# Two of four feed-forward half steps in seven block products for eight

## The chip, the cores and the metric

The kernel runs on one core of a Trainium2 chip. The metric is device microseconds of one execution. TensorE multiplies matrices out of SBUF into PSUM (eight banks of 128 partitions x 2 KB); VectorE, ScalarE and GpSimd work on tiles in SBUF, the first two on PSUM as well; the DMA engines move data between HBM and SBUF. The engines run side by side and wait for each other by semaphores. A framework places the buffers, sets the waits and fixes each engine's order of instructions before the run; an instruction written later in the program can be placed before one written earlier if its inputs are there sooner.

## The reference

Two layers over 544 tokens (512 of a prompt, 8 x 4 of samples), width D = 1024, feed-forward width 2816. Each layer does

```
x = x + 0.5 * SwiGLU_a(RMSNorm(x))
x = x + Mixer(RMSNorm(x))          # layer 0: mLSTM, layer 1: chunk MLP
x = x + 0.5 * SwiGLU_b(RMSNorm(x))
SwiGLU(x) = (silu(x @ w_gate) * (x @ w_up)) @ w_down
```

and a final RMSNorm follows. All in float32. The four SwiGLU half steps are ffn1 and ffn2 of layers 0 and 1; the change touches ffn1 of layer 0 (the first work of the kernel) and ffn2 of layer 1 (the last).

## The kernel before

x lies in SBUF as eight feature tiles of 128 partitions x 544 tokens. For accuracy each matmul operand is split exactly into a high and a low float32r part (`split_into`, L202: ScalarE writes the high part, VectorE subtracts it for the low part), and a product takes three matmuls: high by high, high by low, low by high (`mm3`, L182). PSUM holds a product as two halves of 272 tokens, so each weight block of 128 x 128 makes six matmuls of 272 columns.

`weight` (L146) loads a piece of 128 x 1024 (512 KB) into one of six `raw` slots and splits it into `whi` and `wlo`, two slots each (`WSP`). The norm's gain is multiplied into x before the split (`prep`, L222), squares are summed on ScalarE and GpSimd (`prep_sq`), and the rows' factor `rstd` is applied behind the products (`prep_end`, L236).

`ffn` (L250) goes through 22 hidden tiles in three groups of 8, 8 and 6 (`FF_GROUPS`). For each tile: gate product (48 matmuls), up product (48), then t = gate * rstd on VectorE (L277), SiLU on ScalarE (L278), times rstd on GpSimd (L279), times up on VectorE (L280), and the split of the hidden tile h (L281). Behind a group come eight down products over its tiles; each is added into x (L294), and in the last group x is made ready for the next block (L297). ffn2 of layer 1 ends in `last_down` (L301) and `finish` (L337), which run the last group of down, the final norm and the output. Between the two layers' halves stand `mlstm` (L378), two further half steps with parts of the sample group's state update in between (L1063), and `chunk_mlp` (L970).

PSUM is one pool: two tiles of two banks (`mm`) and four of one bank (`s`). At the start `run` (L1125) loads x, interleaves the first weight piece with it, and splits tile by tile.

Of the kernel before, what the change touches and what calls it, by code (L numbers as in the profile page):

```python
# [17 lines left out]
NT = 544          # 512 prompt tokens, then 8 x 4 sample tokens  # L18
# [26 lines left out]
# columns of the packed per-feature vectors  # L45
# [4 lines left out]
# columns of the packed shape constants  # L50
# [32 lines left out]
def _host(inp):  # L83
# [8 lines left out]

    a = {}
# [6 lines left out]
    for n in ("ffn1", "ffn2"):  # L100
        for w in ("gate", "up", "down"):
            v = f[f"{n}_w_{w}"]
            a[f"{n}_{w}"] = np.stack([wm(v[0]), wm(v[1])])
# [26 lines left out]
class Trunk:  # L130
# [4 lines left out]
    def pool(self, name, bufs=1, space=None):  # L135
        if space is None:
            return self.tc.tile_pool(name=name, bufs=bufs)
        return self.tc.tile_pool(name=name, bufs=bufs, space=space)

# [6 lines left out]
    def weight(self, src=None, raw=None, parts=1):  # L146
        """Loads a piece of a weight matrix and splits it exactly into two float32r parts."""
# [34 lines left out]
    def mm3(self, ps, hi, lo, k0, xs):  # L182
        """ps[half] = sum_k W[k]^T X[k] with both operands in two parts."""
# [10 lines left out]
    def split(self, pool, tag, src, scale=None, n=NT):  # L194
        """Two float32r tiles that sum to src (times a column)."""
# [40 lines left out]
    def prep_end(self):  # L236
# [3 lines left out]
        for h in range(2):  # L240
            c = slice(h * HN, (h + 1) * HN)
            ps = self.st()[:, :HN]
# [7 lines left out]
    def ffn(self, name, l, nextc, side=(), first=None):  # L250
        nc = self.nc
        a = self.a
        with self.pool("ffn") as fp:
# [8 lines left out]
            for gi, (j0, j1) in enumerate(FF_GROUPS):  # L262
                hs = []
                for j in range(j0, j1):
                    gh, gl = first if j == 0 and first else self.weight(a[name + "_gate"][l, j])
# [4 lines left out]
                    uh, ul = self.weight(a[name + "_up"][l, j])  # L270
# [15 lines left out]
                for m in range(KD):  # L286
                    if lastg and nextc is None:
                        self.last_down(a[name + "_down"][l, m][:, j0:j1, :], hs, m)
                        continue
                    dh, dl = self.weight(a[name + "_down"][l, m][:, j0:j1, :])  # L290
# [10 lines left out]
    def last_down(self, src, hs, m):  # L301
        nc, o = self.nc, self.o
        parts = ((0, 256), (256, NT)) if m == KD - 1 else ((0, NT),)
        dh, dl = self.weight(src)
# [5 lines left out]
        x, yt = self.x[m], self.yt  # L310
        if m < KD - 1:
            self.mm3(ps, dh, dl, 0, hs)
        for pi, (t0, t1) in enumerate(parts):
            c = slice(t0, t1)
            if m == KD - 1:
                pv, xv = ps[:, pi, :t1 - t0], x[:, c]
                for k, (xh, xl) in enumerate(hs):
                    for q, (w, h) in enumerate(((dh, xh), (dh, xl), (dl, xh))):
                        nc.tensor.matmul(out=pv, lhsT=w[:, k * P:(k + 1) * P], rhs=h[:, c],
                                         start=k == 0 and q == 0, stop=k == len(hs) - 1 and q == 2)  # L320
            else:
                pv, xv = ps[:, :, :HN], self.v2(x)
# [14 lines left out]
    def finish(self, pi, t0, t1, sq):  # L337
        """The tokens t0 to t1: the rows' sums on the partitions, their factors back across them, the product."""
        nc, o, fin, yt = self.nc, self.o, self.fin, self.yt
        w = (P, 96)[pi]  # L340
# [30 lines left out]
    def dense(self, out, w, i):  # L371
        """out[p, (n d)] = w[p, i, d] where p // 4 == n."""
# [5 lines left out]
    def mlstm(self, nextc):  # L378
        md = self.md
        with self.pool("mlc") as mc:  # L380
# [22 lines left out]
    def phase_a(self):  # L403
        nc, a, o, con = self.nc, self.a, self.o, self.con
        mmt, st = self.mmt, self.st
        with self.pool("pa") as pa:
            self.qkv = pa.tile([P, 3, NI, 4], F32, name="qkv")
            nc.sync.dma_start(out=self.qkv, in_=a["qkv"])
            # the blocks of W_q W_k^T
# [8 lines left out]
            # gate weights through the block-diagonal projections  # L418
# [31 lines left out]
            def post(i, xm):  # L450
# [3 lines left out]
                # causal convolution  # L454
# [19 lines left out]
                # gates  # L474
# [6 lines left out]
                # v and k, tokens on the partitions  # L481
# [23 lines left out]
            def sample(h):  # L505
                """The sample group's q, k and v of a head: rows (feature tile, token), then q and k turned."""
# [30 lines left out]
    def gate_rows(self, pa, gp):  # L537
# [24 lines left out]
        # log sigmoid  # L562
# [39 lines left out]
        # the sample group's values, four times over on the partitions  # L602
# [75 lines left out]
    def norm_cols(self, nq, ecol, stats, n, m):  # L678
        """Columns of the mean of ps and of 1 / std(h) / den, h = ps / den, den = max(|nq|, ecol)."""
# [445 lines left out]
    def run(self):  # L1125
        nc, a, o = self.nc, self.a, self.o
        with self.pool("com") as com, self.pool("xg", 16) as xg, self.pool("hp", 16) as hp, self.pool("wp") as wp, \
# [68 lines left out]
```

## Time and profile before

| | |
|---|---|
| median of 3 runs | 2337.63 us (2336.07 to 2338.55) |
| profiled execution, span | 2334.9 us |
| TensorE, weight loads, VectorE, ScalarE, GpSimd busy | 99%, 95%, 48%, 34%, 15% |
| the four half steps' matmuls | 4 x 3168 of 18076 |

The span runs from the first to the last instruction of one profiled execution; the runs' times have a few microseconds around it. Busy shares are of the span; TensorE's weight loads run beside its matmuls. Read first which engine is full, then whether the chain of work that ended last runs through it, then stretch by stretch whether it waits.

### The profile page before, as it was taken

How to read it: one execution, taken by the hardware profiler on the slowest of the kernel's cores; microseconds unless marked ns; L12 is line 12 of the kernel's file. 1: busy time of each engine (PE TensorE's matmuls, PEld its weight loads, DVE VectorE, ACT ScalarE, POOL GpSimd, SP SyncE). 2: the span in 40 equal slices, each digit the busy share in tenths (PEclk: the TensorE clock that was granted, in tenths of full speed). 3: DMA queues.
4: the chain of work that ended last, by engine and by line, in shares of the span. 5: the costliest groups of instructions: out<-in, count | busy, mean ns of one | idle time of the engine just before them, and what ended most of it. 6: DMA issues, size and time to landing. Idle time of an engine off the chain costs nothing.

```text
span 2334.9 us, 42078 instructions
## 1 busy us (share of the span) xinstructions
PE 2314.8 (99%) x18076; PEld 2220.8 (95%) x18076; DVE 1126.5 (48%) x1642; ACT 787.8 (34%) x1066; POOL 351.5 (15%) x403
## 2 busy tenths in 40 slices
PE   8999999999999999999999999999999999999998
PEld 8999999988987789999999999999999999999998
DVE  5333336543456676644454454545444644333334
ACT  5222123434455453422222342122233433222123
POOL 1101013332111100210111121011121121001011
PEclk9999999999999999999999999999999999999999
DMA  5322223467767663547563444746333223223221
GB/s 179 90 83 91 91 76 110 152 223 233 247 214 259 237 192 102 173 157 265 157 212 118 139 148 157 264 157 210 119 102 96 70 82 91 90 83 91 91 71 59
DMA packets 131089, 337.50 MB, mean 145 GB/s; under 512 B 13168, under 2 KB 26304, under 8 KB 130904
## 3 DMA queue, kind: packets, MB, share of 16 engines
q1 hardware_dynamic: 101152, 276.52, 36.7%
q0 software_dynamic: 9200, 34.02, 4.5%
q10 hardware_dynamic: 20552, 24.29, 2.9%
q8 instruction: 142, 2.33, 0.4%
q14 instruction: 43, 0.35, 0.0%
HBM read 274.97 MB, written 59.81 MB: 143 GB/s over the span
## 4 chain that ended last, share of the span: by engine, by line
PE 95%; DVE 2%; DMA 2%; ACT 1%; issue 0%; POOL 0%; SPq 0%; DVEq 0%; ACTq 0%
PE mm L191 83%; PE mm L926 2%; PE s L191 2%; PE s L719 1%; PE s L497 1%; PE s L853 1%; PE s L889 1%; PE s L1110 1%; DMA xs<-xsd 1%; DMA raw<-in_ml_down 1%; PE s L1040 0%; PE s L836 0%; DVE wlo L206 0%; PE s L478 0%; DVE wg L424 0%
## 5 line engine op out<-in xcount | busy, mean ns | idle before, releaser
L205 ACT ACTIVATE whi<-raw 128x1024 fp32r<-128x1024 f32 (+2 forms) x345 | 358.0, 1038 | 1296.1 <-PE mm L191 1114.4
L191 PE MATMUL mm<-xgh,whi 128*128 128x272 f32 x3744 | 779.7, 289 | 5.8 <-ACT whi L205 5.8
L191 PE MATMUL mm<-xgl,whi 128*128 128x272 f32 x3744 | 776.1, 288 | 0.4 <-DVE xgl L209 0.4
L191 PE MATMUL mm<-xgh,wlo 128*128 128x272 f32 x3744 | 775.1, 288 | 0.0
L191 PEld LDWEIGHTS mm<-xgh,whi 128*128 128x128 f32 x3744 | 588.3, 188 | 23.8 <-issue 14.1
L191 PEld LDWEIGHTS mm<-xgl,whi 128*128 128x128 f32 x3744 | 587.8, 188 | 0.7 <-DVE xgl L209 0.6
L191 PEld LDWEIGHTS mm<-xgh,wlo 128*128 128x128 f32 x3744 | 587.4, 188 | 0.5 <-issue 0.5
L206 DVE TENSOR_TENSOR wlo<-raw,whi 128x1024 fp32r<-128x1024 f32 (+2 forms) x345 | 413.5, 1199 | 63.0 <-ACT whi L205 49.2
L191 PE MATMUL mm<-hh,whi 128*128 128x272 f32 x1508 | 314.2, 289 | 1.3 <-DVE x L294 1.3
L191 PE MATMUL mm<-hl,whi 128*128 128x272 f32 x1508 | 312.2, 288 | 0.0
L191 PE MATMUL mm<-hh,wlo 128*128 128x272 f32 x1508 | 312.0, 288 | 0.1
L279 POOL TENSOR_TENSOR s<-s,rstd 128x544 f32<-128x544 f32 x88 | 151.8, 1726 | 1002.5 <-ACT s L278 1002.5
L191 PEld LDWEIGHTS mm<-hh,whi 128*128 128x128 f32 x1508 | 236.2, 188 | 6.2 <-issue 6.1
L191 PEld LDWEIGHTS mm<-hh,wlo 128*128 128x128 f32 x1508 | 236.5, 188 | 0.8 <-DVE wlo L206 0.8
L191 PEld LDWEIGHTS mm<-hl,whi 128*128 128x128 f32 x1508 | 236.8, 188 | 0.0
L180 DVE TENSOR_TENSOR t<-mm,s 128x544 f32<-128x544 f32 x83 | 60.1, 725 | 331.6 <-PE mm L191 331.6
L294 DVE SCALAR_TENSOR_TENSOR x<-mm,x 128x544 f32<-128x544 f32 x88 | 63.7, 724 | 249.1 <-PE mm L191 249.1
L277 DVE TENSOR_TENSOR t<-mm,rstd 128x544 f32<-128x544 f32 x88 | 63.6, 724 | 240.5 <-PE mm L191 240.4
L1114 DVE SCALAR_TENSOR_TENSOR c<-c,gib,s 128x512 f32<-128x512 f32 x128 | 88.1, 740 | 0.0
L234 POOL TENSOR_TENSOR acc<-acc,sq 128x544 f32<-128x544 f32 x35 | 56.5, 1614 | 175.7 <-ACT sq L233 175.7
L206 DVE TENSOR_TENSOR hl<-t,hh 128x544 fp32r<-128x544 f32 x88 | 63.2, 718 | 2.9 <-ACT hh L205 2.9
L1116 POOL DMA_DIRECT2D out_Cs<-c x32 | 25.0, 782 | 253.4 <-DVE c L1114 246.6
(304 smaller groups left out, 1763.1 us busy)
## 6 DMA issues: line engine op xcount, KB each, us to landing
raw<-in_ffn_up SPq DMA_DIRECT2D x88, 512.0 KB
raw<-in_ffn_gate SPq DMA_DIRECT2D x87, 512.0 KB
raw<-in_ffn_down SPq DMA_DIRECT2D x64, 512.0 KB
c<-in_sC SPq DMA_DIRECT2D x64, 512.0 KB
c<-in_sC SPq DMA_DIRECT2D x32, 1024.0 KB
out_Cs<-c POOLq DMA_DIRECT2D x32, 1024.0 KB, 6.0
raw<-in_ml_up SPq DMA_DIRECT2D x32, 512.0 KB
raw<-in_ffn_down SPq DMA_DIRECT2D x32, 384.0 KB
```

What stands on the lines that cost most here:

```text
L180: self.nc.vector.tensor_tensor(out=self.v2(out), in0=ps[:, :, :HN], in1=self.v2(by), op=ALU.mult)
L191: nc.tensor.matmul(out=ps[h], lhsT=w[:, wsl], rhs=x[:, h * HN:(h + 1) * HN], start=k == 0 and q == 0, stop=k == n - 1 and q == 2)
L205: nc.scalar.activation(out=hi, in_=src, func=AF.Copy)
L206: nc.vector.tensor_tensor(out=lo, in0=src, in1=hi.bitcast(F32), op=ALU.subtract)
L234: (eng or nc.gpsimd).tensor_tensor(out=self.acc, in0=self.acc, in1=sq, op=ALU.add)
L277: nc.vector.tensor_tensor(out=self.v2(t), in0=psg[:, :, :HN], in1=self.v2(self.rstd), op=ALU.mult)
L279: nc.gpsimd.tensor_tensor(out=s, in0=s, in1=self.rstd, op=ALU.mult)
L294: nc.vector.scalar_tensor_tensor(out=xv, in0=ps[:, :, :HN], scalar=0.5, in1=xv, op0=ALU.mult, op1=ALU.add)
L497: nc.tensor.matmul(out=ps[:, tt * P:(tt + 1) * P], lhsT=t[:, tt * P:(tt + 1) * P], rhs=wd[w], start=True, stop=True)
L926: nc.tensor.matmul(out=ps, lhsT=kk[:, tt], rhs=vv[:, tt], start=tt == 0 and q == 0, stop=tt == 3 and q == 2)
L1114: nc.vector.scalar_tensor_tensor(out=c0[:, r, :], in0=c0[:, r, :], scalar=self.gib[:, h, b:b + 1], in1=ps[r], op0=ALU.mult, op1=ALU.add)
L1116: nc.gpsimd.dma_start(out=self.pair(o["Cs"], v)[:, h, dsl].rearrange("r p e -> p r e"), in_=c0)
```

## The change

Strassen's scheme in Winograd's form. A 2 x 2 block of weight tiles (two feature blocks by two) times a pair of feature tiles is made of seven block products in place of eight. The sums of weight blocks are formed on the chip: B21 + B11 and B21 + B22 by DMAs that add into SBUF (issued on GpSimd, behind a plain load of B21), one on VectorE and one on GpSimd. The sums of x and of the hidden tiles (T1 to T4) are formed on VectorE; all seven are split into high and low parts. The recombination is done in PSUM: a partial result is copied by ScalarE from one bank to another, and later products add to it there; before, eight matmuls with zeros have touched all banks (`arm`). The two token halves play the part of the right operand's columns, so each matmul is still 128 x 128 by 272. PSUM is two sets of four banks in these half steps and the old two kinds elsewhere (`psum`); pools of SBUF tiles change with the stage (`x_pool`). Groups have 3, 3, 3 and 2 blocks (`SV_GROUPS`, a block is two hidden tiles). The last group of down at the very end is done by ordinary products (`last_down`). The first weight piece is no longer loaded ahead of x. The other two half steps, the mLSTM and the chunk MLP keep their work, but for `hp` opened later and one split there.

```diff
+SEVEN = {("ffn1", 0), ("ffn2", 1)}
+SV_GROUPS = ((0, 3), (3, 6), (6, 9), (9, 11))
+ADDS = "dma"
+B11, B21, B22, T4, T1, T2, T3, B12 = range(8)
...
     def prep(self, k):
+        if self.xkind == "s":
+            if k % 2:
+                self.px[k // 2] = self.sums_x(k - 1)
+            self.prep_sq(k)
+            return
...
+    def arm(self):
+        sets = [self.set(), self.set()]
+        for t in sets:
+            for b in range(4):
+                self.nc.tensor.matmul(out=t[:, b, :HN], lhsT=self.onesr, rhs=self.zeros, start=True, stop=True)
+
+    def set(self):
+        return self.pp.tile([P, 4, 512], F32, tag="set", name="set", bufs=2)
+
+    def sums(self, t, hi, lo, parts=1):
+        nc = self.nc
+        nc.vector.tensor_tensor(out=t[:, T1:T3 + 1:2], in0=t[:, B12:B12 + 1].to_broadcast([P, 2, HN]),
+                                in1=t[:, B11:B22 + 1:2], op=ALU.subtract)
+        nc.vector.tensor_tensor(out=t[:, T2], in0=t[:, B22], in1=t[:, T1], op=ALU.subtract)
+        nc.vector.tensor_tensor(out=t[:, T4], in0=t[:, B21], in1=t[:, T2], op=ALU.subtract)
+        for c in ((slice(0, 7),) if parts == 1 else (slice(0, 3), slice(3, 7))):
+            self.split_into(hi[:, c], lo[:, c], t[:, c])
+        return hi, lo
+
+    def sums_x(self, k):
...
+        t = self.ht.tile([P, 8, HN], F32, tag="hT", name="hT", bufs=1)
...
+        return self.sums(t, hi, lo, 2)
+
+    def weight_sums(self, src):
...
+        ta, tb, tc = (raw(self.wp, "raw", 2, RAW) for _ in range(3))
+        td = raw(self.wx, "rawd", 1, 2)
+        nc.sync.dma_start(out=ta[:, 0], in_=b11)
+        if ADDS == "dma":
+            nc.sync.dma_start(out=ta[:, 1], in_=b21)
+            nc.sync.dma_start(out=tc[:, 1], in_=b21)
+            nc.gpsimd.dma_start(out=ta[:, 1], in_=b11, accum_op=ALU.add)
+            nc.gpsimd.dma_start(out=tc[:, 1], in_=b22, accum_op=ALU.add)
+            nc.sync.dma_start(out=tb[:, 0], in_=b12)
+            nc.sync.dma_start(out=tc[:, 0], in_=b22)
...
+        nc.vector.tensor_tensor(out=tb[:, 1], in0=tc[:, 1], in1=ta[:, 0], op=ALU.add)
+        nc.gpsimd.tensor_tensor(out=td[:, 0], in0=tb[:, 1], in1=tb[:, 0], op=ALU.add)
+        out = []
+        for t in (ta, tb, tc):
+            hi, lo = (self.wp.tile([P, 2, 512], F32R, tag=g, name=g, bufs=WSP)[:, :, :n] for g in ("whi", "wlo"))
+            self.split_into(hi, lo, t)
+            out += [(hi[:, i], lo[:, i]) for i in range(2)]
+        hi, lo = (self.wx.tile([P, 512], F32R, tag=g, name=g, bufs=1)[:, :n] for g in ("whd", "wld"))
+        self.split_into(hi, lo, td[:, 0])
+        return out + [(hi, lo)]
+
+    def seven(self, t, src, xs, scale=1.0, sums=None):
+        nc = self.nc
+        w11, w7, w12, w6, w22, w5, w3 = self.weight_sums(src)
+        bank = [t[:, b, :HN] for b in range(4)]
...
+        product(0, w11, B11, True)
+        nc.scalar.activation(out=bank[2], in_=bank[0], func=AF.Copy, scale=-1.0)
+        product(1, w7, T3, True)
+        e = self.wx.tile([P, HN], F32, tag="e", name="e", bufs=2)
+        nc.scalar.activation(out=e, in_=bank[1], func=AF.Copy, scale=scale)
+        product(2, w6, T2, False)
+        nc.scalar.activation(out=bank[3], in_=bank[2], func=AF.Copy)
+        product(0, w12, B21, False)
+        product(3, w5, T1, False)
+        nc.scalar.activation(out=bank[1], in_=bank[3], func=AF.Copy, scale=-1.0)
+        product(2, w22, T4, False)
+        product(1, w3, B22, False)
+        return e.unsqueeze(1).to_broadcast([P, 2, HN])
+
+    def ffn_seven(self, name, l, nextc, start=False):
...
+            for gi, (j0, j1) in enumerate(SV_GROUPS):
+                lastg = gi == len(SV_GROUPS) - 1
+                hs = []
+                for j in range(j0, j1):
+                    t = self.set()
+                    e = self.seven(t, gate[j], xs)
+                    s = ht.tile([P, 2, 2, HN], F32, tag="s", name="s", bufs=1)
+                    u = self.set()
+                    if j == 0:
+                        self.prep_end([u[:, 2, :HN], u[:, 3, :HN]])
+                    r2 = self.v2(self.rstd)
+                    nc.vector.tensor_tensor(out=s[:, 0], in0=t[:, 0:2, :HN], in1=r2, op=ALU.mult)
+                    nc.vector.tensor_tensor(out=s[:, 1], in0=t[:, 2:4, :HN], in1=e, op=ALU.add)
+                    nc.vector.tensor_tensor(out=s[:, 1], in0=s[:, 1], in1=r2, op=ALU.mult)
+                    nc.scalar.activation(out=s, in_=s, func=AF.Silu)
+                    nc.gpsimd.tensor_tensor(out=s.rearrange("p a b c -> p a (b c)"),
+                                            in0=s.rearrange("p a b c -> p a (b c)"),
+                                            in1=self.rstd.unsqueeze(1).to_broadcast([P, 2, NT]), op=ALU.mult)
+                    e = self.seven(u, up[j], xs)
+                    h = ht.tile([P, 8, HN], F32, tag="hT", name="hT", bufs=1)
+                    nc.vector.tensor_tensor(out=h[:, B11:B12 + 1:B12 - B11], in0=u[:, 0:2, :HN], in1=s[:, 0],
+                                            op=ALU.mult)
+                    nc.vector.tensor_tensor(out=h[:, B21:B22 + 1], in0=u[:, 2:4, :HN], in1=e, op=ALU.add)
+                    nc.vector.tensor_tensor(out=h[:, B21:B22 + 1], in0=h[:, B21:B22 + 1], in1=s[:, 1], op=ALU.mult)
...
+                    hs.append(self.sums(h, hi, lo))
...
+                for m in range(KD // 2):
+                    t = self.set()
+                    e = self.seven(t, down[m][:, :, j0:j1], hs, scale=0.5)
...
             self.prep_begin(C_FF1)
-            for k in range(KD):
-                self.px[k] = self.split(self.xg, "xg", self.x[k], scale=self.col(C_FF1 + k))
-                if k == 0:
-                    first = self.weight(raw=raw, parts=2)
...
-            self.ffn("ffn1", 0, C_MIX, first=first)
+            self.psum("s")
+            self.ffn_seven("ffn1", 0, C_MIX, start=True)
+            self.psum("c")
             self.mlstm(C_FF2)
```

## Rows read from the trace of the kernel before

**Rows 1.** The page, part 1: busy time of each engine, share, instructions.

```profile
PE 2314.8 (99%) x18076; PEld 2220.8 (95%) x18076; DVE 1126.5 (48%) x1642; ACT 787.8 (34%) x1066; POOL 351.5 (15%) x403
```

**Rows 2.** The page, part 4: the chain that ended last, by engine.

```profile
PE 95%; DVE 2%; DMA 2%; ACT 1%; issue 0%; POOL 0%; SPq 0%; DVEq 0%; ACTq 0%
```

**Rows 3.** Stretches: PE, PEld, DVE, ACT, POOL busy us, clock, DMA share, GB/s.

```profile
0.00:22.00 22.00, 15.72 (x108) 15.07 (x109) 15.50 (x25) 16.85 (x25) 0.41 (x5) 1.00 0.88 330
148.00:244.00 96.00, 96.00 (x767) 96.00 (x766) 35.50 (x39) 25.37 (x30) 12.39 (x7) 1.00 0.29 88
...
365.00:415.00 50.00, 48.59 (x378) 47.46 (x377) 38.48 (x101) 20.77 (x30) 20.68 (x26) 1.00 0.41 123
```

**Rows 4.** Timeline from 98 us, TensorE and VectorE: start, us, engine, line.

```profile
97.93 0.41 PE L191 MATMUL mm<-xgh,whi 128*128 128x272 f32 x2
...
99.19 0.41 PE L191 MATMUL mm<-xgh,wlo 128*128 128x272 f32 x2
...
99.64 0.72 DVE L277 TENSOR_TENSOR t<-mm,rstd 128x544 f32<-128x544 f32 x1 [3.27 <-PE mm L191]
...
104.96 0.41 PE L191 MATMUL mm<-xgl,whi 128*128 128x272 f32 x2
```

**Rows 5.** Groups by line and shape, whole span: busy us, mean ns, idle before.

```profile
L206 DVE TENSOR_TENSOR wlo<-raw,whi 128x1024 fp32r<-128x1024 f32 x311 | 381.0, 1225 | 62.7 <-ACT whi L205 48.9
L205 ACT ACTIVATE whi<-raw 128x1024 fp32r<-128x1024 f32 x311 | 329.7, 1060 | 1220.6 <-PE mm L191 1068.3 <-issue 75.5 <-DMA raw<-in_ml_up 27.3
...
L277 DVE TENSOR_TENSOR t<-mm,rstd 128x544 f32<-128x544 f32 x88 | 63.6, 724 | 240.5 <-PE mm L191 240.4
...
L208 ACT ACTIVATE xgh<-x,cols 128x544 fp32r<-128x544 f32 x48 | 35.3, 746 | 20.8 <-DVE x L294 11.5 <-DVE x L960 4.6 <-PE mm L191 2.0
L206 DVE TENSOR_TENSOR wlo<-raw,whi 128x768 fp32r<-128x768 f32 x32 | 31.1, 973 | 0.0
L205 ACT ACTIVATE whi<-raw 128x768 fp32r<-128x768 f32 x32 | 27.0, 844 | 75.5 <-PE mm L191 46.0 <-issue 29.3
...
L1116 POOL DMA_DIRECT2D out_Cs<-c x32 | 25.0, 782 | 253.4 <-DVE c L1114 246.6 <-DVE wlo L206 6.8
...
L206 DVE TENSOR_TENSOR hl<-raw,hh 128x512 fp32r<-128x512 f32 x16 | 10.8, 686 | 4.6 <-ACT hh L205 4.6
...
L424 DVE TENSOR_TENSOR wg<-wg,qkv 128x32 f32<-128x32 f32 x48 | 9.9, 268 | 0.0
...
L205 ACT ACTIVATE hh<-raw 128x512 fp32r<-128x512 f32 x16 | 9.3, 625 | 4.4 <-DMA raw<-xsd 3.8 <-ACT sz L675 0.5
...
L245 ACT ACTIVATE rstd<-s,eps 128x272 f32<-128x272 f32 x12 | 5.2, 484 | 0.1
...
L178 DVE TENSOR_TENSOR t<-s 128x272 f32<-128x272 f32 x10 | 3.9, 435 | 8.3 <-POOL s L279 8.3
...
L1101 POOL DMA_DIRECT2D out_ns<-sn x4 | 2.3, 566 | 17.6 <-DVE sn L1099 17.6
```

**Rows 6.** Timeline from 394 us: weights' low parts on VectorE beside GpSimd.

```profile
396.44 0.30 PEld L191 LDWEIGHTS mm<-hh,wlo 128*128 128x128 f32 x2 [0.26 <-DVE wlo L206]
...
400.39 0.95 DVE L206 TENSOR_TENSOR wlo<-raw,whi 128x768 fp32r<-128x768 f32 x1
...
401.95 1.36 POOL L234 TENSOR_TENSOR acc<-acc,sq 128x544 f32<-128x544 f32 x1 [3.59 <-ACT sq L233]
...
402.62 1.50 DVE L206 TENSOR_TENSOR wlo<-raw,whi 128x768 fp32r<-128x768 f32 x1
```

**Rows 7.** Timeline of the start, TensorE and ScalarE.

```profile
5.77 0.82 PE L191 MATMUL mm<-xgh,whi 128*128 128x272 f32 x2 [5.77 <-ACT whi L205]
...
5.98 0.75 ACT L208 ACTIVATE xgh<-x,cols 128x544 fp32r<-128x544 f32 x1 [0.26 <-DMA x<-in_xT]
...
10.14 0.41 PE L191 MATMUL mm<-xgh,whi 128*128 128x272 f32 x2
```

**Rows 8.** The page, part 6: GpSimd's DMAs, KB each, us to landing.

```profile
out_Cs<-c POOLq DMA_DIRECT2D x32, 1024.0 KB, 6.0
```

More of the change, by code (lines that the diff above doesn't have):

```diff
@@ L1 @@
+import contextlib
 import numpy as np
@@ L91, in wm, with pairs @@
         return w.reshape(k // P, P, m // P, P).transpose(2, 1, 0, 3)
+    def pairs(w):
+        k, m = w.shape
+        t = w.reshape(k // 256, 2, P, m // 256, 2, P).transpose(3, 2, 4, 1, 0, 5)
+        return np.stack([t[:, :, i, j] for i, j in ((0, 0), (0, 1), (1, 1), (1, 0))], 2)
     a = {}
@@ L101, in _host @@
         for w in ("gate", "up", "down"):
-            v = f[f"{n}_w_{w}"]
-            a[f"{n}_{w}"] = np.stack([wm(v[0]), wm(v[1])])
+            for l in range(2):
+                a[f"{n}{l}_{w}"] = (pairs if (n, l) in SEVEN else wm)(f[f"{n}_w_{w}"][l])
     a["ml_up"] = wm(f["ml_w_up"][0])
@@ L234, in prep_sq, with prep_end @@
             (eng or nc.gpsimd).tensor_tensor(out=self.acc, in0=self.acc, in1=sq, op=ALU.add)
-    def prep_end(self):
+    def prep_end(self, sums=None):
         nc = self.nc
@@ L241, in prep_end @@
             c = slice(h * HN, (h + 1) * HN)
-            ps = self.st()[:, :HN]
+            ps = sums[h] if sums else self.st()[:, :HN]
             for q in range(2):
@@ L264, in ffn @@
                 for j in range(j0, j1):
-                    gh, gl = first if j == 0 and first else self.weight(a[name + "_gate"][l, j])
+                    gh, gl = first if j == 0 and first else self.weight(a[f"{name}{l}_gate"][j])
                     psg = self.mmt()
@@ L286, in ffn @@
                 for m in range(KD):
[L287 to L290, printed above, removed]
+                    dh, dl = self.weight(a[f"{name}{l}_down"][m][:, j0:j1, :])
                     ps = self.mmt()
@@ new lines, in seven, with product @@
+    def seven(self, t, src, xs, scale=1.0, sums=None):
+        nc = self.nc
+        w11, w7, w12, w6, w22, w5, w3 = self.weight_sums(src)
+        bank = [t[:, b, :HN] for b in range(4)]
+        def product(b, w, i, start):
+            z, last = 0, 3 * len(xs) - 1
+            for k, (xh, xl) in enumerate(xs):
+                c = slice(k * P, (k + 1) * P)
+                for ww, xx in ((w[0], xh), (w[0], xl), (w[1], xh)):
+                    nc.tensor.matmul(out=bank[b], lhsT=ww[:, c], rhs=xx[:, i], start=start and z == 0, stop=z == last,
+                                     skip_group_check=True)
+                    z += 1
+        product(0, w11, B11, True)
[11 more added lines that the diff above has]
+        return e.unsqueeze(1).to_broadcast([P, 2, HN])
@@ L305, in last_down @@
+    def last_down(self, src, m, j0, j1, hs):
+        nc, o = self.nc, self.o
+        parts = ((0, HN), (HN, NT))
+        nj = j1 - j0
+        raw = self.raw(n=2 * nj * P).rearrange("p (a b) -> p a b", a=2)
+        for k in range(2):
+            nc.sync.dma_start(out=raw[:, k], in_=src[:, (0, 1, 3, 2)[2 * (m % 2) + k], j0:j1].rearrange("p a b -> p (a b)"))
+        wh, wl = self.weight(raw=raw.rearrange("p a b -> p (a b)"))
         ps = self.mmt()
@@ L310, in last_down, with half @@
         x, yt = self.x[m], self.yt
+        def half(pi):
+            z = 0
+            for k in range(2 * nj):
+                w0 = (k % 2 * nj + k // 2) * P
+                xh, xl = hs[k]
+                for w, h in ((wh, xh), (wh, xl), (wl, xh)):
+                    nc.tensor.matmul(out=ps[:, pi, :HN], lhsT=w[:, w0:w0 + P], rhs=h[pi],
+                                     start=z == 0, stop=z == 6 * nj - 1)
+                    z += 1
         if m < KD - 1:
-            self.mm3(ps, dh, dl, 0, hs)
-        for pi, (t0, t1) in enumerate(parts):
+            half(0)
+            half(1)
+        for pi, (t0, t1) in enumerate(parts if m == KD - 1 else ((0, NT),)):
             c = slice(t0, t1)
             if m == KD - 1:
[L316 to L320, printed above, removed]
+                half(pi)
+                pv, xv = ps[:, pi, :HN], x[:, c]
             else:
@@ L379, in mlstm @@
         md = self.md
-        with self.pool("mlc") as mc:
+        with self.pool("hp", 16) as self.hp, self.pool("mlc") as mc:
             def dram(shape, name):
@@ L1144, in run @@
             nc.vector.memset(self.eps, EPS)
-            late = com.tile([P, 1], F32, name="late")
-            nc.scalar.activation(out=late, in_=self.eps, func=AF.Copy)
             self.mhalf = com.tile([P, 4], F32, name="mhalf")
```

115 lines of the change are left out of this document (91 added, 24 removed).

## The prediction

> **What bounds the kernel now.** I read the engine totals first, then the chain of work that ended last, then stretches of the span, then single instructions. TensorE is busy 99% of the span while VectorE, ScalarE and GpSimd have 48, 34 and 15% [rows 1], and 95% of the chain is TensorE [rows 2]. Inside a half step nothing waits: in 148 to 244 us TensorE is busy all 96.00 us, VectorE 35.50, GpSimd 12.39, and the DMA engines 0.29 [rows 3]. So a matmul removed there is time removed, as long as the others keep up. The pace: the pairs that start at 97.93 and at 104.96 us lie 56 matmuls apart, 0.1255 us for one [rows 4]. Each matmul already has a weight load of its own, 18076 to 18076 [rows 1], so the same 128x272 form with other weights each time should keep that pace.
>
> **What is removed.** A half step has 3168 matmuls: 22 gate and 22 up tiles of 48, and 8 x 22 x 6 for down. With seven products the gate or up tile pair takes 84 in place of 96, and a down pair of three blocks 63 in place of 72. ffn1 of layer 0 becomes 22 x 84 + 12 x 63 + 4 x 42 = 2772. ffn2 of layer 1 keeps ordinary products for its last two blocks of down: 22 x 84 + 12 x 63 + 192 = 2796. That is 396 + 372 = 768 fewer, times 0.1255 = **-96.4 us**. Zeroing the eight banks twice adds 16 matmuls, **+2**.
>
> **What is added on the other engines, per tile pair of gate and up** (two calls of `seven`, 168 matmuls, 21.1 us of TensorE). Durations from [rows 5]; per element a low part takes (1225 - 686)/512 = 1.05 ns more and a high part 0.85, so 1904 elements are 2.15 and 1.81 us.
> VectorE: weights' low parts 6 x 1.225 + 2 x 0.686 = 8.7; two sums of 512, 1.4; six steps on s and h of 544, 0.72 each, 4.3; the differences of h, 0.72 + 2 x 0.435 = 1.6; h's low part 2.15. Sum **18.2 us** of 21.1, against some 9 of 24.1 now (four weight low parts, six steps of 0.72).
> ScalarE: 6 x 1.06 + 2 x 0.625 = 7.6; eight PSUM copies of 272, between 0.42 (the 512's 0.625 less 240 elements) and the 0.48 of the nearest row, a square root from PSUM, which I take, 3.9; the SiLU of 1088, 1.1; h's high part 1.8. Sum 14.4.
> GpSimd: two sums of 512 (about 1.3 each undisturbed) and a product of 1088, twice the 1.36 that an undisturbed 544 takes [rows 6], so 5.3, and four DMA issues of 0.57 to 0.78 [rows 5].
> DMA: seven pieces of 256 KB for a `seven` in place of four tiles' worth; 1.8 MB in 10.5 us is about twice today's 88 GB/s [rows 3], far from the 330 of the first stretch. I take the traffic as free; the adding DMAs are a rival below.
>
> **One call of `seven`, laid out.** Products start every 12 x 0.1255 = 1.51 us. A result is read 0.2 us behind its slot: the last pair of a product starts at 99.19, its slots end at 99.44, VectorE reads at 99.64 [rows 4]. The third product waits for a ScalarE copy of the first: 0.2 + 0.48 + 0.1 against 1.51, slack 0.7, if ScalarE isn't inside a 1.06 or 1.81 us instruction; the fifth and the seventh wait in the same way for a copy. Each engine's order is fixed before the run and not shown in this trace; behind a waiting copy stand ScalarE's next high parts. The third weight tile takes over the first one's slot (two slots): free at 3.0, high part from 3.1 to 4.2, low part to 5.4, needed at 6.0 to 6.3. Slack under 1 us. Where the gate call runs beside the h chain of the tile pair before, h's high part (1.81) or low part (2.15) lands in one of those slacks and costs 0.5 to 1.6 us; the up call, beside the SiLU and the 2.7 us GpSimd product, about 0.4. A measured relative: in 365 to 415 us, with VectorE at 38.48 of 50 and GpSimd at 20.68, TensorE falls to 48.59, so 2.8% goes [rows 3], in waits on a low part such as the 0.26 at 396.44 [rows 6]. At 86% and with less slack I take 1.7 us for a tile pair, bounds 0.5 and 3.5: 22 x 1.7 = **+37 us** (11 to 77).
> A down call has 1.13 us products, so the copy's slack is 0.3 and the third tile's (0.84 + 0.97 [rows 5]) about 0.2: 0.5 for each of 24 (0.2 to 1); in the last group of ffn1 four calls of 5.3 us carry about 6.8 us of VectorE work, for they also split x: 1.7 each. **+19 us** (6 to 36).
>
> **The end of a group.** Now a group has 8, 8 or 6 tiles, so down begins with 42 or 30 matmuls that don't need the last one. With groups of three, two or so blocks, only 6 (0.75 us) go ahead. Behind the last up product come: read delay 0.2, h 0.72, differences 1.6, high part 1.8, low part 2.15, hand-overs 0.3; 6.8 less 0.75 and a little of the next product leaves 5.7. Nothing else can fill it: both weight slots hold down's first tiles. Seven groups (four in ffn1, three in ffn2; the eighth has no differences): **+40 us** (32 to 49).
>
> **The start.** Now the matmuls run at half pace from 5.77 and in full from about 10 us [rows 7]; 108 in the first 22 us [rows 3] are 13.6 us of work, so it is as if they had begun at 8.4. After: four pairs of x go one behind another through one buffer, each two scaled copies (1.5), differences 1.6, the second high part 1.1, the second low part 1.3 and hand-overs, 5.8 us. The first ends about 5 us behind its second x tile (5.98 [rows 7]), at 11, the fourth at 28.4, and the weights, now queued behind x with an adding DMA on top, come at about 18. By 28.4 some two products (3 us) are done: as if begun at 25.4 to 28 with squares and sums in between. **+20 us** (14 to 25).
>
> **Small ones.** From the chunk MLP into ffn2 the last x pair takes its copies, differences and splits, about 6 us, with 2.2 us of matmuls ahead of it, in place of a cover of 42: +5 (3 to 8). Last down: its first tiles wait for the last h and the banks, +3 (2 to 5). The mLSTM's own weight preparation, of which the 48 steps of 0.27 alone are 9.9 us of VectorE [rows 5], today fills gaps in 365 to 415 us (the 38.48 above) and will meet a full VectorE: +4 (0 to 15). The last chunk-MLP split to another pool: nothing, its slots have long been free.
>
> **Sum.** -96.4 + 2 + 37 + 19 + 40 + 20 + 5 + 3 + 4 = **+33.6 us**. The profiled execution spans 2334.9 us; 2.7 more lie around it up to the median of 2337.63 (runs 2336.07 to 2338.55). I forecast 2334.9 + 33.6 + 2.7 = **2371 us**.
>
> **Rivals.**
> A: the covers hold. All terms at their lower bounds: 11 + 6 + 32 + 14 + 3 + 2 + 0 + 2 = 70, so -26, **2311 us**. For it: an order of work fixed ahead can put the copies and the third tile's split first, and VectorE has 3 us to spare in each tile pair. Against: drain and start alone are 46 of it, and no engine can shorten them.
> B: VectorE and GpSimd shut each other out. A 768 low part takes 0.95 us alone; one that starts at 402.62, while GpSimd adds from 401.95 to 403.31, takes 1.50, as if it had begun when GpSimd ended [rows 6]. Two-input SBUF steps on VectorE are 8.7 + 1.4 + 1.4 + 1.6 + 2.15 = 15.3 of the 18.2; with GpSimd's 5.3 they fill 20.6, and the 2.9 us that read PSUM hide only in part: 22 to 23.5 a tile pair against 21.1, plus imperfect packing. At 3.5 us lost per tile pair: 77 in place of 37, **2411 us**. It decides once the mean gap of a tile pair passes about 2.5 us. The Trainium skill, "SBUF — State Buffer", section "Who interferes with whom", says that a VectorE instruction with two SBUF inputs and a GpSimd instruction that reads SBUF exclude each other for the whole instruction. By that the time would be B's; the row at 402.62 agrees with it.
> C: the adding DMAs come late. In the trace a GpSimd DMA of 1 MB lands in 6.0 us [rows 8], and no adding one is shown. A weight's way is load, issue, adding DMA, sum, sum, split, with two calls (21 us) of buffers ahead. Each waits on GpSimd for its plain load, and behind it there stand the sums and the SiLU product; behind VectorE's sum stand the low parts. If such a DMA took over 10 us, both queues would block: at 1.5 us for each of 72 calls +108, **2479 us**. Bounds: 0 to that. It decides when gaps of TensorE end on a sum fed by DMA.
>
> **How the numbers follow.** Forecast (2340 to 2400) 0.40, A 0.36, B 0.14, C 0.10. About 0.2% is what a measurement of this kernel can tell from no change: 2333 to 2342. A lies nearly whole below it (some 2285 to 2337), the forecast's lower edge touches it: faster 0.34, same 0.06, slower 0.60. The range reaches into A and through B: 2295 to 2440, which leaves out A's fast end and C. The forecast's own, 2340 to 2400.
>
> **What would show it.** Right: TensorE's matmul count falls by about 750; VectorE near 85% and ScalarE near 65% in the two changed half steps; in each group a TensorE gap of 5 to 6 us that ends on h's low part; first full pace past 25 us; gaps of about a microsecond ending on a copy or a low part; the two unchanged half steps and the mLSTM as long as before. Wrong: no gap at the group ends (something fills them), a matmul pace other than 0.1255, gaps ending on an adding DMA, or a gate and up stretch in which TensorE never waits.

## The result: 2757.85 us, 18% longer

The changed kernel takes 2757.85 us (median; 2752.53 to 2775.12) against 2337.33 for the kernel before on the same chip: a ratio of 1.1812, 95% interval 1.1777 to 1.1848. That is 387 us beyond the forecast and 318 beyond the upper end of the range. The profiled execution spans 2758.5 us. Its page, part 1 (busy time, share, instructions), and the row of part 2 with the granted clock in 40 slices, to be laid beside [rows 1]:

```profile
PE 2404.4 (87%) x17336; PEld 2231.9 (81%) x17336; DVE 1441.8 (52%) x2015; ACT 1023.3 (37%) x1486; POOL 586.4 (21%) x604
...
PEclk9989887978999999999999999999999898989888
```

The 740 matmuls are gone, yet TensorE is busy 90 us longer and idle 354 us in place of 20. No other engine is full, and every slice with a clock below 9 lies in a changed half step or holds its end or its start. By stage, from marks on the timeline: the first half step's products end at 640.8 us in place of 410.0 (+231). From there to the chunk MLP's last update of x it is 1523.9 in place of 1513.2 (+11). From there to the end it is 593.8 in place of 411.7 (+182). So +424, nearly all of it in the two changed half steps.

What TensorE waits for, the same kernel (what waits <- what it waits for: us in total, times, longest us; L425, L428, L430 and L433 are the four ScalarE copies inside a call of `seven`, L241 and L242 the high and low parts):

```profile
PE set L421 <- ACT e L428: 117.0, 72, 3.7
PE set L421 <- ACT set L430: 53.8, 72, 2.5
PE set L421 <- ACT hh L241: 41.6, 7, 6.0
PE set L421 <- ACT set L425: 33.4, 71, 0.5
PE set L421 <- ACT whi L241: 19.4, 1, 19.4
PE set L421 <- DVE wlo L242: 17.6, 15, 2.6
PE set L421 <- ACT set L433: 17.1, 60, 0.5
PE set L421 <- DVE hl L242: 11.1, 7, 1.6
```

There are 72 calls of `seven`, and most wait for all four copies (60 to 72 times each): 221 us. The group ends (`hh` and `hl`, seven each) are 52.7. Inside one call, on the timeline of TensorE (start, duration, ..., idle before and its releaser):

```profile
2643.00 0.29 PE L421 MATMUL set<-hh,wld 128*128 128x272 f32 x1
2645.53 0.59 PE L421 MATMUL set<-xsh,wlo 128*128 128x272 f32 x1 [2.24 <-DVE wlo L242]
2645.92 0.43 PE L421 MATMUL set<-xsh,whi 128*128 128x272 f32 x1
2646.15 0.43 PE L421 MATMUL set<-xsl,whi 128*128 128x272 f32 x1
...
2648.64 0.60 PE L421 MATMUL set<-xsh,whi 128*128 128x272 f32 x1 [0.47 <-ACT set L425]
...
2652.93 0.40 PE L421 MATMUL set<-xsh,whi 128*128 128x272 f32 x1 [1.21 <-ACT e L428]
...
2655.24 0.39 PE L421 MATMUL set<-xsh,whi 128*128 128x272 f32 x1 [0.53 <-ACT set L430]
...
2659.06 0.39 PE L421 MATMUL set<-xsh,whi 128*128 128x272 f32 x1 [0.28 <-ACT set L433]
```

The four rows with a copy behind the arrow are the starts of products 2, 3, 4 and 6. None of the four needs the copy that it waits for: product 2 writes bank 1 while L425 copies bank 0 into bank 2; product 3 adds to bank 2 while L428 reads bank 1; product 4 adds to bank 0 while L430 copies bank 2 into 3; product 6 adds to bank 2 while L433 copies bank 3 into 1. All four banks are one PSUM tile, `set`, and the waits here go by tile. Products 3, 5 and 7, which do need a copy, find it made.

After the gap of 2.24 us the matmuls follow each other by 0.23 us in place of 0.1255. Stretches of the same kernel, matmuls of L421 alone (us, PE busy, PEld busy, clock, DMA share, GB/s):

```profile
2640.14:2643.10 2.96, 2.85 (x21) 2.60 (x20) 1.00 0.77 141
2645.50:2651.50 6.00, 5.50 (x22) 5.08 (x22) 0.50 0.58 174
2653.20:2654.60 1.40, 1.40 (x12) 1.29 (x11) 1.00 0.85 104
```

The granted clock is 0.50, 1.2 GHz for 2.4, behind the idle 2.24 us, and 1.00 again by 2653.2. Over the kernel, some 750 matmuls in 36 such stretches cost about 75 us more than at 0.1255 each, and some 240 single matmuls behind short gaps another 25.

### The profile page after: what moved, and what is told of

It is laid out like the page before. It is cut to its first block, busy times and chain, and to the rows that moved or that the text cites. A ratio compares the mean times of both kernels' runs of the same rounds, so it can differ in the third digit from the quotient of the medians.

```text
span 2758.5 us, 42692 instructions
## 1 busy us (share of the span) xinstructions
PE 2404.4 (87%) x17336; PEld 2231.9 (81%) x17336; DVE 1441.8 (52%) x2015; ACT 1023.3 (37%) x1486; POOL 586.4 (21%) x604
## 5 line engine op out<-in xcount | busy, mean ns | idle before, releaser
L241 ACT ACTIVATE whi<-raw 128x1024 fp32r<-128x1024 f32 (+2 forms) x432 | 429.9, 995 | 1124.3 <-PE mm L227 650.7
L242 DVE TENSOR_TENSOR wlo<-raw,whi 128x1024 fp32r<-128x1024 f32 (+2 forms) x432 | 525.6, 1220 | 348.9 <-ACT whi L241 338.7
L421 PE MATMUL set<-xsh,whi 128*128 128x272 f32 x1056 | 347.5, 329 | 174.8 <-ACT e L428 82.6
L227 PE MATMUL mm<-xgh,whi 128*128 128x272 f32 x2368 | 494.4, 290 | 0.2 <-DVE x L1175 0.2
L227 PE MATMUL mm<-xgl,whi 128*128 128x272 f32 x2368 | 490.5, 288 | 0.7 <-DVE xgl L245 0.7
L227 PE MATMUL mm<-xgh,wlo 128*128 128x272 f32 x2368 | 489.7, 288 | 0.0
L421 PEld LDWEIGHTS set<-xsh,whi 128*128 128x128 f32 x1056 | 221.1, 209 | 216.0 <-ACT e L428 92.8
L227 PEld LDWEIGHTS mm<-xgl,whi 128*128 128x128 f32 x2368 | 371.3, 188 | 1.0 <-DVE xgl L245 1.0
L421 PE MATMUL set<-xsh,wlo 128*128 128x272 f32 x1056 | 328.8, 311 | 14.1 <-DVE wlo L242 14.1
L421 PE MATMUL set<-xsl,whi 128*128 128x272 f32 x1056 | 328.1, 311 | 3.1 <-DVE xsl L242 3.1
L421 PE MATMUL set<-hh,whi 128*128 128x272 f32 x480 | 170.7, 356 | 111.1 <-ACT hh L241 41.6
L421 PEld LDWEIGHTS set<-xsh,wlo 128*128 128x128 f32 x1056 | 222.5, 211 | 16.4 <-DVE wlo L242 16.4
L421 PEld LDWEIGHTS set<-xsl,whi 128*128 128x128 f32 x1056 | 223.1, 211 | 4.0 <-DVE xsl L242 4.0
L421 PEld LDWEIGHTS set<-hh,whi 128*128 128x128 f32 x480 | 107.4, 224 | 139.7 <-ACT hh L241 43.2
L421 PE MATMUL set<-hl,whi 128*128 128x272 f32 x480 | 157.0, 327 | 11.1 <-DVE hl L242 11.1
```

The costliest lines, as they stand in the source:

```text
L227: nc.tensor.matmul(out=ps[h], lhsT=w[:, wsl], rhs=x[:, h * HN:(h + 1) * HN], start=k == 0 and q == 0, stop=k == n - 1 and q == 2)
L241: nc.scalar.activation(out=hi, in_=src, func=AF.Copy)
L242: nc.vector.tensor_tensor(out=lo, in0=src, in1=hi.bitcast(F32), op=ALU.subtract)
L421: nc.tensor.matmul(out=bank[b], lhsT=ww[:, c], rhs=xx[:, i], start=start and z == 0, stop=z == last, skip_group_check=True)
```

## The experiments

The times are medians. All ratios are to the kernel before; where one kernel is set against another, the difference is between medians.

**Theories at the start.** W: products wait for copies of banks that they don't touch, because the four banks are one tile. D: the adding DMAs hold the weights back (rival C of the prediction). L: VectorE and GpSimd shut each other out (rival B).

**e1_banks**: four tiles of one bank in place of one of four; VectorE's two-bank steps become two each (not in the diff).

```diff
-        return self.pp.tile([P, 4, 512], F32, tag="set", name="set", bufs=2)
+        return [self.pp.tile([P, 512], F32, tag=f"set{b}", name="set", bufs=2)[:, :HN] for b in range(4)]
```

> Only the PSUM tiles change: each set of four banks is four tiles of one bank, and the steps that read two banks at once are two. In the changed kernel a product starts only when ScalarE's copy written ahead of it is done, even where the copy touches other banks. Theory W (waits by tile): those four waits of a call (273 us over both half steps beyond the matmuls' own time) shrink to under 60 us, and with the gaps most of the half-pace stretches (about 100 us with the restarts) go too: 2430 us, between 2385 and 2490. Rival D (the adding DMAs are late): nothing about them changes, 2700 to 2760. Rival L (VectorE and GpSimd shut each other out): VectorE gets about 2 us more a tile pair, 2700 to 2800.

2562.97 us, ratio 1.0971 [1.0955, 1.0987]: 195 less. No product waits for L428 or L433 any more; those for L425 and L430, which some products do need, are left. It is still above what theory W gave, for a new wait heads the list:

```profile
PE set L421 <- DVE wlo L242: 109.7, 59, 5.2
...
PE set L421 <- ACT set L430: 18.3, 14, 2.4
PE set L421 <- ACT set L425: 13.9, 13, 1.9
```

Its cause, on the timelines of VectorE, SyncE, GpSimd and ScalarE in this kernel (start, duration, ..., idle before and releaser):

```profile
142.98 1.69 DVE L242 TENSOR_TENSOR wlo<-raw,whi 128x768 fp32r<-128x768 f32 x1
144.74 0.33 SPq L386 DMA_DIRECT2D raw<-in_ffn_gate  x1
148.98 0.87 POOL L388 DMA_DIRECT2D raw<-in_ffn_gate  x1 [3.81 <-DVE wlo L242]
149.16 0.84 ACT L241 ACTIVATE whi<-raw 128x768 fp32r<-128x768 f32 x1 [0.55 <-PE set L421]
154.70 0.69 DVE L398 TENSOR_TENSOR raw<-raw 128x512 f32<-128x512 f32 x1 [5.59 <-DMA raw<-in_ffn_gate]
155.53 1.26 POOL L399 TENSOR_TENSOR rawd<-raw 128x512 f32<-128x512 f32 x1 [5.69 <-DVE raw L398]
155.66 1.95 DVE L242 TENSOR_TENSOR wlo<-raw,whi 128x768 fp32r<-128x768 f32 x1
```

An adding DMA adds to a plain load of B21 (L386). SyncE can request that load only when VectorE's low part of an earlier weight (142.98 to 144.67) has freed the raw slot: 144.74. It lands at 148.41, and GpSimd issues the adding DMA at 148.98. (The low part in that row's bracket ended by chance just before: of the 18 issues of L388 from 120 to 360 us, 16 stand 0.56 to 0.57 us behind the landing of their load.) VectorE's sum, next in its fixed order, waits for it in front of the queue until 154.70, 5.7 us later. The high part made from 149.16 gets its low part at 155.66, though its inputs were there at 150.0. So the way is a ring of 10 us: VectorE's low part, the plain load, the adding DMA, VectorE's sum, and behind it the next low part.

**e2_adds and e3_banks_adds**: the two sums by GpSimd and VectorE in place of adding DMAs, on the changed kernel and on e1.

```diff
-ADDS = "dma"
+ADDS = "eng"
```

> Only the two adding DMAs of each call go: B21 is loaded once, one sum is made on GpSimd (some 1.3 us), one on VectorE (0.7 us). Theory W: the waits on the copies stay, so 2740 to 2830. Rival D: the DMA wait goes with the DMAs, at least 100 us less, under 2650. Rival L: 72 calls with 2 us more of excluding work, 2800 to 2900.

> Both edits together: one-bank PSUM tiles, and the weight sums on GpSimd and VectorE in place of adding DMAs. Theory W: near the one-bank kernel, with VectorE and GpSimd fuller 0 to 80 us more: 2430 to 2510. Rival D: well below the one-bank kernel, by 50 us or more. Rival L: above the one-bank kernel by more than 80 us.

e2: 2727.75, 1.1665 [1.1645, 1.1684], 30 less than the changed kernel. e3: 2438.69, 1.0433 [1.0417, 1.0448], 124 less than e1 and 289 less than e2. So the adding DMAs cost 30 us behind the copies' waits and 124 without those: each hides part of the other. e2 lies just under theory W's range; e3 lies in W's and meets D's too, for both hold.

**e4_sum_pool**: e1, with the sum behind the adding DMAs on GpSimd (of the two results it reads one, `tc[:, 1]`; the other, in `ta[:, 1]`, is a weight as it stands).

```diff
-        nc.vector.tensor_tensor(out=tb[:, 1], in0=tc[:, 1], in1=ta[:, 0], op=ALU.add)
+        nc.gpsimd.tensor_tensor(out=tb[:, 1], in0=tc[:, 1], in1=ta[:, 0], op=ALU.add)
```

> The one-bank version with the two adding DMAs kept, and only the sum that consumes both of their results (tb[:, 1] = tc[:, 1] + ta[:, 0]) moved from VectorE's queue to GpSimd's. Theory Q (VectorE's fixed order is what costs: that sum heads the queue waiting for an adding DMA, 5.6 us in the run with one-bank tiles, while the low parts of finished tiles stand behind it): most of the 124 us between the one-bank version with adding DMAs (2563.0) and the one with engine sums (2438.7) comes back, 2450 to 2500, and the matmuls' waits for VectorE's low parts (109.7 us in 59 gaps) fall under 50. Rival (the adding DMAs make the weight itself late, whichever engine does the sum): 2530 or more, the waits for low parts stay near 110.

2469.69, 1.0568 [1.0552, 1.0584]; the waits for low parts fall from 109.7 to 43.3 us:

```profile
PE set L421 <- DVE wlo L242: 43.3, 24, 5.9
```

One instruction on another queue takes back 93 of the 124 us with the same DMAs. The move also spares VectorE 72 sums; e6 below leaves out 144 and gains 21 us, so that is the smaller part. Mostly it was not the DMA that was slow for its consumer, but its consumer that stood in front of others.

**e5_no_pool, e6_no_dve_sums, e7_drain**, each against e3: what is left? Without GpSimd's tensor steps; without VectorE's two weight sums; the parts of a group's last h in two pieces. One line stands for each (e5 also leaves out GpSimd's other sum and its product, e6 VectorE's other sum).

```diff
-            nc.gpsimd.tensor_tensor(out=ta[:, 1], in0=ta[:, 0], in1=t21[:, 0], op=ALU.add)
+            nc.sync.dma_start(out=ta[:, 1], in_=b21)
...
-            nc.vector.tensor_tensor(out=tc[:, 1], in0=tc[:, 0], in1=t21[:, 0], op=ALU.add)
+            nc.sync.dma_start(out=tc[:, 1], in_=b22)
...
-                    hs.append(self.sums(h, hi, lo))
+                    hs.append(self.sums(h, hi, lo, 2 if j == j1 - 1 else 1))
```

> The version with one-bank tiles and engine sums (2438.7), with GpSimd's three tensor steps of the changed half steps left out (the sum td, the sum ta, which is a plain load instead, and the product of SiLU and 1/rms), so its output is another one. Theory L (what is left of the loss per tile pair, 3.2 us, is VectorE made slower by GpSimd's steps: a low part of 1.50 us beside them against 0.95 alone in the kernel before): the 22 tile pairs fall by 1.5 to 3 us each, 2370 to 2405. Rival (what is left is the order of products, copies and splits within the call): at most 10 us less, 2428 to 2440.

> The version with one-bank tiles and engine sums (2438.7), with VectorE's two weight sums per call left out (plain loads in their place, 72 calls, two more transfers of one block each on SyncE's queue), so its output is another one. Theory V (VectorE, 88 per cent busy in the changed half steps, is what is left of the loss; two sums of about 0.7 us each per call): calls fall by 0.7 to 1.4 us where a low part ends the gaps, 2340 to 2390. Rival (VectorE is not the end of the path; products wait for ScalarE's copies and high parts): at most 15 us less, 2424 to 2440.

> The version with one-bank tiles and engine sums (2438.7), with the high and low parts of the last h of each group made in two pieces (three sums first, then four), so that the first products of the group's down calls can start on the first piece. Theory (the seven group ends cost 8.7 us each because the whole chain of differences and parts of the last h stands between the up call and the down call): about 2 us less at each of seven group ends, and 5 to 14 us less in all with the clock kept up, 2425 to 2434. Rival (the down call's weights, which are split behind h on the same engines, come last): no change, 2436 to 2442.

e5: 2388.14, 1.0219 [1.0204, 1.0235], 51 less: theory L. e6: 2417.45, 1.0345 [1.0329, 1.0360], 21 less, between what theory V and its rival expected: VectorE's sums matter, but not first. e7: 2427.59, 1.0389 [1.0372, 1.0406], 11 less. What GpSimd does to VectorE, in groups by line and shape in 120 to 400 us of e3 (busy us, mean ns, idle before):

```profile
L397 DVE TENSOR_TENSOR raw<-raw,raw 128x512 f32<-128x512 f32 x16 | 19.3, 1205 | 9.0 <-issue 7.5 <-DVE x L496 0.9 <-DMA raw<-in_ffn_gate 0.6
L242 DVE TENSOR_TENSOR wld<-rawd,whd 128x512 fp32r<-128x512 f32 x14 | 16.1, 1150 | 0.0
```

and of e5, where the same steps stand on L396 and L242:

```profile
L396 DVE TENSOR_TENSOR raw<-raw,raw 128x512 f32<-128x512 f32 x16 | 11.0, 689 | 8.1 <-DMA raw<-in_ffn_gate 6.4 <-DMA raw<-in_ffn_up 1.7
L242 DVE TENSOR_TENSOR wld<-raw,whd 128x512 fp32r<-128x512 f32 x16 | 10.9, 682 | 0.0
```

The same sum takes 689 ns with GpSimd quiet and 1205 beside it, the seventh weight's low part 682 and 1150. The means of e3 mix two kinds. Of these sums and low parts, the 15 that no GpSimd step touches take 0.68 to 0.69 us. The 15 that begin inside one all end 0.55 us behind its end, as if they had begun when it was done. One of them in e3:

```profile
170.23 2.54 POOL L464 TENSOR_TENSOR s<-s,rstd 128x1088 f32<-128x1088 f32 x1
170.63 2.69 DVE L397 TENSOR_TENSOR raw<-raw,raw 128x512 f32<-128x512 f32 x1 [2.08 <-issue]
```

Here the Trainium skill, "SBUF — State Buffer", section "Who interferes with whom", is borne out as in [rows 6].

**e9_all_vec and e8_floor.** e9 is e7 with GpSimd's three steps given to VectorE. e8 is e7 without any weight sums and without the product of SiLU and 1/rms.

```diff
-            nc.gpsimd.tensor_tensor(out=ta[:, 1], in0=ta[:, 0], in1=t21[:, 0], op=ALU.add)
+            nc.vector.tensor_tensor(out=ta[:, 1], in0=ta[:, 0], in1=t21[:, 0], op=ALU.add)
...
-        nc.gpsimd.tensor_tensor(out=td[:, 0], in0=tb[:, 1], in1=tb[:, 0], op=ALU.add)
+        nc.vector.tensor_tensor(out=td[:, 0], in0=tb[:, 1], in1=tb[:, 0], op=ALU.add)
...
-                    nc.gpsimd.tensor_tensor(out=s.rearrange("p a b c -> p a (b c)"),
+                    nc.vector.tensor_tensor(out=s.rearrange("p a b c -> p a (b c)"),
```

> The version with one-bank tiles, engine sums and the last h of each group in two pieces (2427.6), with GpSimd's three tensor steps of the changed half steps (the sums ta and td, the product of SiLU and 1/rms) moved to VectorE: nothing is left out, only the engine changes. Theory L (GpSimd's steps cost VectorE about what VectorE would need to do them itself: its sum of 128x512 took 1205 ns beside them and 689 ns without them, its low part of the seventh weight 1150 and 682): VectorE's busy time stays within 40 us of e7_drain's 1574.8 although it gets some 120 us of work, and the kernel takes 2395 to 2425. Rival V (VectorE is bound by its count of instructions, and each added one lengthens the calls): VectorE's busy time rises by 80 us or more and the kernel takes 2440 to 2490.

> A floor for the scheme in this kernel: one-bank tiles, the last h of each group in two pieces, and all four weight sums and GpSimd's product of SiLU and 1/rms left out (the sums are plain loads), so its output is another one; seven products, their copies, and the splits into high and low parts stay. If the single savings add up (50.6 without GpSimd's steps, 21.2 without VectorE's sums, 11.1 from the two pieces, from 2438.7): 2350 to 2362. If they overlap, because with GpSimd quiet VectorE's sums are no longer last: 2365 to 2385. Under 2336 would say that the seven products themselves can pay here once the sums cost nothing; over it, that start, group ends and the order inside a call cost more than the 96 us of matmuls even then.

e9: 2364.33, 1.0125 [1.0110, 1.0140], 63 less than e7 and better than either theory gave. The page, part 1, of e7:

```profile
PE 2279.4 (94%) x17336; PEld 2158.6 (89%) x17336; DVE 1574.8 (65%) x2238; ACT 1020.5 (42%) x1493; POOL 538.4 (22%) x532
```

and of e9:

```profile
PE 2263.6 (96%) x17336; PEld 2153.0 (91%) x17336; DVE 1554.9 (66%) x2404; ACT 1022.3 (43%) x1493; POOL 286.5 (12%) x366
```

VectorE has 166 instructions more and is busy 20 us less; GpSimd is relieved of 252. Sharing the work out had cost VectorE more than doing it. GpSimd is also the slower for these steps (e3 in 120 to 400 us: a sum 1484 ns, the product 2577; VectorE in e9: 686 and 1289). How much of e5's 51 and e9's 63 us comes from that, and how much from the exclusion, no run separates. e8: 2341.24, 1.0020 [1.0010, 1.0031]: the savings add up and more, yet with all weight sums and that product free the scheme in two half steps still doesn't beat eight products.

**e11_one_tile**: e9 with the four-bank tile put back; nothing else differs.

```diff
-        return [self.pp.tile([P, 512], F32, tag=f"set{b}", name="set", bufs=2)[:, :HN] for b in range(4)]
+        t = self.pp.tile([P, 4, 512], F32, tag="set", name="set", bufs=2)
+        return [t[:, b, :HN] for b in range(4)]
```

> The version with everything on VectorE (2364.3), with the four-bank product tile of the change put back, so that a product waits for ScalarE's copies of banks that it doesn't touch; nothing else changes. If that tile costs what it cost between the two versions with engine sums (2727.8 against 2438.7, 289 us): 2640 to 2690. Rival (a part of those 289 us was VectorE and GpSimd being late behind the same gaps, so that quieter engines leave less): 2500 to 2600.

2701.15, 1.1561 [1.1545, 1.1577]: 337 more, above what both theories gave. Its waits:

```profile
PE set L422 <- ACT e L429: 119.3, 72, 3.7
PE set L422 <- ACT set L431: 38.2, 72, 0.5
PE set L422 <- ACT set L426: 33.7, 72, 0.5
...
PE set L422 <- ACT set L434: 17.1, 59, 0.6
```

In e9 the list has of these four only:

```profile
PE set L421 <- ACT set L430: 19.4, 15, 2.2
...
PE set L421 <- ACT set L425: 6.5, 9, 1.9
```

Weights, sums and splits are in time in e11: low parts of weights hold TensorE for 4.4 us in all. The tile alone costs 337 / 72 = 4.7 us a call. Of it the four waits are 208 us in all, against 26 in e9. What matmuls at 1.2 GHz and behind short gaps take beyond 0.1255 each is some 94 against 23. Of the remaining 84, about 45 may be the end of the last matmul ahead of each of the 275 gaps (an estimate: idle time counts from a matmul's end, 0.29 us after its start, and not from its slot of 0.1255, so 0.16 a gap); the rest stays open.

**e10_last_only**: e9 with the scheme in the last half step alone.

```diff
-SEVEN = {("ffn1", 0), ("ffn2", 1)}
+SEVEN = {("ffn2", 1)}
...
-            self.ffn_seven("ffn1", 0, C_MIX, start=True)
+            with self.pool("hp", 16) as self.hp:
+                self.ffn("ffn1", 0, C_MIX, first=first)
```

> The version with everything on VectorE (2364.3), with the scheme in the last half step only; the first half step is that of the kernel before. In the profiles, the stretch from the last update of x in the chunk MLP to the end lasts 411.7 us in the kernel before, 408.5 in the version with everything on VectorE, 593.8 in the changed kernel. If stages add, 3 us less than before: 2329 to 2337. Rival (the gain of the last half step hangs on the first one's layout, or the changed pools cost the first half step something): 2340 to 2350.

2331.52, 0.9978 [0.9968, 0.9988]: 5 us (0.2%) less than the kernel before, the only version here that is faster. The last stretch, from the chunk MLP's last update of x (1922.24 us) to the end of its span of 2329.6 us, takes 407.4 against 411.7. So what e9 still loses lies ahead of that: its first half step ends at 433.6 us for 410.0, and the middle stretch is 8 us longer. The copy behind its first product stands at 38.05 us, so its late start (below: 28 us) is more than that half step's whole loss.

## Why the prediction was wrong, point by point

**The step that failed** is in the call laid out: "The third product waits for a ScalarE copy of the first ... the fifth and the seventh wait in the same way for a copy". I took waits from the banks that are read and written. The change keeps four banks in one tile, and the waits were made for the tile, so products 2, 3, 4 and 6 wait for a copy of the product just ahead, with no slack at all. The prediction named gaps "of about a microsecond ending on a copy or a low part" as a sign of being right; for a wait at nearly every product it had no rival. Shown by e1 (-195), e3 against e2 (-289) and e11 (+337, nothing else changed). The trace of before has the sign in one place, which the prediction didn't use. At its very end VectorE reads bank 0 of the tile `mm`, and matmuls for bank 1 of the same tile are next on TensorE (L345 is another tile's):

```profile
2319.50 0.41 DVE L323 SCALAR_TENSOR_TENSOR x<-mm,x 128x256 f32<-128x256 f32 x1
2319.64 0.38 PE L345 MATMUL s<-ones,acc 128*128 128x1 f32 x2 [0.20 <-DVE acc L331]
2319.97 0.40 PE L319 MATMUL mm<-hh,whi 128*128 128x288 f32 x1
```

The first matmul into bank 1 starts 0.06 us behind the end of the read, and its weight load waits for VectorE's semaphore, though both operands have long been in use. The pools of the changed kernel also have an option that the printed diff leaves out, `reuse_waits="tile"`, and no run varies it; the kernel before has no such option and waits in the same way.

The Trainium skill, "Perfetto Trace Analysis", section "Optimizing Tensor Performance", asks that independent groups of matmuls go round through different PSUM banks so that an eviction runs beside the next group. The change does go round its banks, and its trace shows 221 us of waits; only with a tile for each bank did the evictions run beside the products.

**What a gap costs** was counted as the gap alone. In the kernel before TensorE hardly ever stands still, and the clock is 0.998 of full speed; after, it is 0.945 and 100 us go to slow matmuls.

**Tile pair, 1.7 us** (0.5 to 3.5). From one L425 copy to the next, the two calls of a pair take 15.75 + 17.32 us in the changed kernel, nominally 21.08: 12.0 lost. In e3, without the copies' waits and with one sum more a call on VectorE and on GpSimd than I had counted, 12.38 + 11.91: 3.2 lost. That is near rival B's 3.5, and e5 (22.2, 1.1 lost), without GpSimd's steps, says that they carry most of it. e9, with still more on VectorE and nothing on GpSimd, loses 1.0. So the load was not the trouble, and I had put what GpSimd's steps cost too low.

**Down calls, +19** (0.5 us each, 1.7 in ffn1's last group): between two calls of three blocks 5.1 us are lost in the changed kernel, 0.4 in e3 and 1.4 in e9. In ffn1's last group, which also splits x, e3 loses 3.3 a call.

**Rival C** was right in kind, wrong in its condition: "over 10 us". Adding DMAs of 256 KB land in 5.1 to 5.5 us (DMA issues of the changed kernel), less than [rows 8] for four times as much, and still cost 124 us in e1. I counted "two calls (21 us) of buffers ahead", but a slot comes free only with the low part of an earlier weight, and then a plain load (3.7 us in the rows of e1) and the adding DMA (5.7) follow one behind the other.

**Group ends, +40** (32 to 49): right in place and cause, too low in size. The waits for `hh` and `hl` are 52.7 us in the changed kernel and 41.1 in e3. From mark to mark e3 loses 9.1 at each, slow matmuls among them, for 5.7 predicted. With two pieces e7 loses 3.4 and e9 1.6, though I had written that nothing could fill this gap. Much of it moved, however: e7 takes 40 us off the seven ends but only 11 off the kernel, since the down calls behind them now lose 1.8 each in place of 0.4.

**Start, +20** (14 to 25): too low. The first real matmul comes at 22.95 us, and the copy behind the first product at 38.33. It is as if the products had begun at 36.6 (0.2 and 1.5 earlier), 28 us later than before. Waits for a weight's low part, for parts of x and for the norm's factor (1.7 to 2.8 us each between 23 and 37 us) hold the first product open.

**The rest**: from the chunk MLP into ffn2 the gap is 6.9 us in e9 (5 predicted, 3 to 8). The middle stretch grew by 11 us, in e9 by 8 (mLSTM's preparation, +4, 0 to 15); in e9 that is one gap of 8.0 us of TensorE up to 456.15, in which VectorE works through the 48 steps. The matmul count and the pace of 0.1255 wherever nothing waits were right, so the -96 us is real (740 matmuls are 93 us). But VectorE's 85% came only once the copies were out of the way: in 120 to 400 us it is 49% busy in the changed kernel, 85% in e3, 91% in e9.

**Sum.** Of the 421 us between the medians, e1, e3, e7 and e9 in turn take back 195, 124, 11 and 63, and 27 remain. Since the effects hide each other, that is one order of undoing, not a division: put back last, the tile alone is worth 337. e9's own terms (tile pairs 23, group ends 11, down calls 39, start 28, chunk MLP into ffn2 7, middle 8, less 93 for 740 matmuls) make 23 of its 28. That is near the forecast's +34, but from terms of other sizes: that the totals are near is luck.

## What to carry to other kernels

Fewer matmuls pay only while the waits that come with them cost less: before cutting a saturated engine's work, list for each new wait which buffer the framework tracks (here the whole tile, not the bank), and give each bank that is read while its neighbour is written a tile of its own. An instruction that consumes a late DMA belongs on a queue where nothing urgent stands behind it. Work split between VectorE and GpSimd can cost VectorE more than doing all of it, so compare the duration of the same instruction with and without a neighbour first.

## What the hardware showed that was not expected

An idle TensorE of 2.24 us was followed by 22 matmuls at a granted clock of 0.50, 0.23 us each in place of 0.1255, and full speed came back by 2653.2 us. In the half steps of the kernel before, matmuls follow each other so slowly in a row only in its first 10 us [rows 7]. Behind a gap of 0.3 to 0.5 us the first matmul alone takes 0.23 us until the next one starts, with full pace behind it (2655.24 and 2659.06). An adding DMA of 256 KB from GpSimd's queue landed in 5.1 to 5.5 us, one of 128 KB in 3.1 (medians in the changed kernel). A VectorE sum of two SBUF inputs begun inside a GpSimd step ended 0.55 us behind that step's end, 15 times out of 15 (e3).
